# TensorE's order pinned to the written order through the whole retention of a hybrid decoder block

## The chip, the cores and the metric

The kernel runs on one core of one Trainium2 chip. The metric is the device time of one execution in microseconds. Before the change it is 1546.49 us, the median of 3 runs (1546.46 to 1546.75). Everything is float32 data of one sequence of 1024 tokens, model width 1024, one layer.

## What is computed

The layer normalises x, makes one combined projection, runs two branches on it (a retention with 4 heads, and a sliding-window attention), merges them through gates and ends with a SwiGLU feed-forward. The change lies in the retention. There the sequence is cut into 8 chunks of 128 tokens, and a state of 128 x 256 is carried from chunk to chunk:

```python
def step(state, inp):
    qn, kn, vn = inp
    scores = jnp.einsum('bhcd,bhsd->bhcs', qn, kn) * intra_decay
    inner = jnp.einsum('bhcs,bhse->bhce', scores, vn)
    cross = jnp.einsum('bhcd,bhde->bhce', qn, state) * q_decay
    new_state = state * chunk_decay + jnp.einsum('bhsd,bhse->bhde', kn * k_decay, vn)
    return new_state, inner + cross
...
ry = head_group_norm(ry, ret_norm_g[l]).astype(x.dtype)
branch_a = (jax.nn.silu(rg) * ry) @ w_ret_out[l]
...
branch_b = ay.reshape(B, S, ATTN_Q) @ w_attn_out[l]
merged = jax.nn.sigmoid(gate_a) * branch_a + jax.nn.sigmoid(gate_b) * branch_b
```

## The kernel before

Every large product keeps float32 accuracy by splitting each operand into a high part (a cast on ScalarE, `nc.scalar.copy`) and a low part (a subtraction on VectorE), and by three TensorE products (high x high, high x low, low x high) that add up in one PSUM bank. So each value that leaves PSUM and enters a product again passes ScalarE and then VectorE.

The stage around the change is the retention, which follows a stage of weight products (`wproduct`, L1022). That stage ends with results of the gates: `wresult` (L975) adds two parts on VectorE (L1002), takes a tanh on ScalarE (L1009) and stores the result to HBM (L1010, issued from SyncE's queue). Its result tile `r` has two buffers, so the add of one block waits until the store of the block two before has landed. In the same place the second half of the attention result, `ay`, is loaded in two transfers of 2048 KB each (L1048).

Then comes, for head 0, `load_g(0)` and `k_transpose(0)` (L1156): 8 transposes on TensorE into the two banks of PSUM tag `t` (tiles `kTT`), each bank then cast by ScalarE (L1165) and subtracted by VectorE (L1166). Only after both has the bank been read for the last time.

Each head is a generator `core(h)` (L1168 to 1305). Its steps on TensorE are: `scores` (L1194, tile `rs`, a bank of tag `t`), four times `states` (L1185 to 1187 into tile `u`), four times `outputs` (the same lines, into tile `y`), twice `gated` (transposes `yT`, L1258, bank `t`), and `k_transpose` of the next head. `scores` first runs four matmuls into its bank; VectorE multiplies them with the mask (L1197, `sm`), and the halves `smh`, `sml` go into `outputs`. Between the steps the generator yields a number, 3 or 4.

The yields are filled by `Fill` (L208) with the products of `w_attn_out` (`bb_g`, L1141; lines 178 to 180, tile `acc_bb`). A filling step is three matmuls of 128 x 512. There are 8 x 16 = 128 of them, and the yields of the four heads ask for 4 x 32 = 128. They need only `ay` and their own weights `wh_bb`, `wl_bb`, not the retention.

What sets the order: each engine runs its own list of instructions strictly in its order. A scheduler makes that list from the written program, by its own estimate of when operands are ready. Where the code stands within `in_order(engine)` (L117), each instruction of that engine is tied to the one before it as written, and the scheduler can move nothing there. Before, `pinned = in_order(nc.tensor.engine)` opens at L1107 and closes at L1309, just after `k_transpose(0)`. From there on the scheduler chooses TensorE's order. VectorE, ScalarE and SyncE's queue are left to the scheduler in the retention in both kernels.

Of the kernel before, what the change touches and what calls it, by code (L numbers as in the profile page):

```python
# [40 lines left out]
def hybrid_block(ctx: ExitStack, tc: tile.TileContext, x, ln1_g, w_in, b_in, ret_norm_g, w_ret_out,  # L41
# [74 lines left out]
    @contextmanager  # L116
    def in_order(*engines):  # L117

        traced = nc.cur_bb.bb.instructions
        last = traced[-1]  # L120
        yield
        start = next(k for k in reversed(range(len(traced))) if traced[k] is last) + 1
        prev = {}
        for i in traced[start:]:
            if i.engine in engines:
                if i.engine in prev:
                    tc.add_manual_dep(i, prev[i.engine],
                                      mybir.DependencyInfo(mybir.DependencyClass.NoSync, mybir.DependencyReason.DATA),
                                      reason="in_order")
                prev[i.engine] = i.name  # L130
# [53 lines left out]
    def run(gen):  # L184
        for _ in gen:
            pass
# [920 lines left out]
    pinned = in_order(nc.tensor.engine)  # L1107
# [33 lines left out]
    def bb_g(n):  # L1141
        def evac(half, pt):
            c = slice(half * 512, half * 512 + 512)
            t = rt.tile([P, 512], F32, tag="r", bufs=2, name=f"tbr{n}{half}")
            nc.sync.dma_start(t, tb_d[8 + n, :, c])
            m = w2.tile([P, 512], F32, tag="mbw", bufs=1, name=f"mb{n}{half}")
            nc.vector.scalar_tensor_tensor(out=m, in0=t, scalar=1.0, in1=pt, op0=ALU.add, op1=ALU.mult)
            nc.sync.dma_start(mb_d[n, :, c], m)
        return dense_g(w_attn_out, n * P, AY, evac, f"bb{n}")
# [6 lines left out]
    def k_transpose(h):  # L1156
        kt = [w2.tile([P, NB, P], F32R, tag=f"kt{z}", bufs=1, name=f"kt{h}{z}") for z in range(2)]
        kts[h] = kt
        for q in range(2):
            pt = ps("t", 2, f"kTT{h}{q}")  # L1160
            for i in range(4):
                nc.tensor.transpose(pt[:, i * P:(i + 1) * P], kTs[h][:, (q * 4 + i) * P:(q * 4 + i + 1) * P], ident)
            ptv = pt.rearrange("p (c d) -> p c d", c=4)
            hi, lo = (z[:, q * 4:q * 4 + 4, :] for z in kt)
            nc.scalar.copy(hi, ptv)  # L1165
            nc.vector.tensor_tensor(out=lo, in0=ptv, in1=f32(hi), op=ALU.subtract)  # L1166
# [139 lines left out]

    load_g(0)
    k_transpose(0)
    pinned.__exit__(None, None, None)  # L1309
    fl = Fill([bb_g(n) for n in range(8)])  # L1310
    last = None
    for h in range(RH):
# [10 lines left out]
        last = gen  # L1323
    fl.rest()
    run(last)
    w2c.__exit__(None, None, None)
    rtc.__exit__(None, None, None)
    kqc.__exit__(None, None, None)
# [804 lines left out]
```

## Time and profile before

| | before |
|---|---|
| time, median of 3 runs | 1546.49 us |
| the profiled execution, its own time | 1546.24 us |
| its span, first to last instruction | 1544.1 us |
| TensorE (PE) busy | 1532.1 us, 99% |
| VectorE (DVE) busy | 1024.5 us, 66% |
| ScalarE (ACT) busy | 693.5 us, 45% |
| GpSimd (POOL) busy | 386.3 us, 25% |
| mean granted TensorE clock | 0.999 |

The profile is one execution taken by the hardware profiler. Times in its timeline are microseconds from the start of the span. In a row of the timeline stand the start, the duration, the engine, the line of the kernel, the operation, output and inputs, the shape, and in brackets the idle time before it with what ended it. PEld is TensorE's weight load, SPq is SyncE's queue of DMA issues. A matmul is listed with its whole passage, so the spacing of the starts, not the duration, is what it takes from the engine. An `x8` on four float32 matmuls of 128 x 128 means that each is carried out as two.

### The profile page before, as it was taken

The numbers are of one execution on the slowest core, as the hardware profiler recorded it, in microseconds if no ns is written. First come the engines' busy times: TensorE is split into PE (matmuls) and PEld (weight loads), VectorE is DVE, ScalarE is ACT, GpSimd is POOL, SyncE is SP. The second block draws the span as 40 slices with busy tenths as digits, with TensorE's granted clock in tenths as the row PEclk, the third lists the DMA queues.
The fourth block names the chain that finished last, engine by engine and source line by source line (L and its number), as shares of the span: only waits on it lengthen the run. The fifth ranks groups of instructions, "written<-read, shape, count | busy, mean of one in ns | idle before, by whom it ended". The sixth has DMA issues, their size and how long they took to land.

```text
span 1544.1 us, 20386 instructions
## 1 busy us (share of the span) xinstructions
PE 1532.1 (99%) x7299; PEld 1279.8 (83%) x7299; DVE 1024.5 (66%) x1590; ACT 693.5 (45%) x1368; POOL 386.3 (25%) x344
## 2 busy tenths in 40 slices
PE   9999999999999999999999999999999999999998
PEld 8888878888888888888888888888888888888886
DVE  7588897884677764887558688444444444688666
ACT  6366666332344454544223465333333333344445
POOL 2011111002233320000120216555555555100001
PEclk9999999999999999999999999999999999999999
DMA  6656474315766647653657103333333333963332
GB/s 229 187 163 189 144 250 166 103 55 175 207 195 196 213 163 262 206 192 117 204 178 253 68 1 123 109 103 103 102 103 103 103 104 108 318 226 96 92 111 118
DMA packets 158001, 236.85 MB, mean 153 GB/s; under 512 B 10603, under 2 KB 81069, under 8 KB 157645
## 3 DMA queue, kind: packets, MB, share of 16 engines
q1 hardware_dynamic: 155292, 227.04, 45.7%
q0 software_dynamic: 2560, 8.39, 1.5%
q8 instruction: 57, 0.93, 0.3%
q14 instruction: 44, 0.35, 0.1%
q10 hardware_dynamic: 48, 0.13, 0.0%
HBM read 156.62 MB, written 74.19 MB: 149 GB/s over the span
## 4 chain that ended last, share of the span: by engine, by line
PE 94%; DVE 3%; DMA 1%; issue 1%; ACT 1%; SPq 0%; POOL 0%; POOLq 0%; DVEq 0%
PE fA L1757 16%; PE wA L1022 8%; PE fB L1757 8%; PE dA L2059 7%; PE dxP L2059 6%; PE wB L1022 4%; PE fC L1757 4%; PE va L865 3%; PE wo L1591 3%; PE woP L1591 2%; PE wC L1022 2%; PE vP L865 2%; PE aq L178 2%; PE aq L179 2%; PE aq L180 2%; PE acc_ba L180 2%
## 5 line engine op out<-in xcount | busy, mean ns | idle before, releaser
L2059 PE MATMUL dA<-dwP,daP 128*128 128x512 f32 x528 | 120.6, 389 | 0.0
L2059 PEld LDWEIGHTS dA<-dwP,daP 128*128 128x128 f32 x528 | 99.0, 188 | 20.7 <-DVE dwP L154 0.2
L2059 PE MATMUL dxP<-dwP,daP 128*128 128x512 f32 x396 | 90.2, 389 | 0.0
L2059 PEld LDWEIGHTS dxP<-dwP,daP 128*128 128x128 f32 x396 | 74.3, 188 | 15.4
L1832 POOL TENSOR_TENSOR xf<-xf 128x512 f32<-128x512 f32 x40 | 63.9, 1598 | 31.0 <-issue 28.8
L734 POOL TENSOR_TENSOR wr_wp<-wr_wp 128x512 f32<-128x512 f32 x12 | 18.2, 1514 | 193.5 <-DVE w0P L154 92.5
L642 POOL DMA_DIRECT2D xy_d<-xy x32 | 23.1, 723 | 157.2 <-ACT xy L641 98.9
L1763 POOL TENSOR_TENSOR xf<-xf 128x512 f32<-128x512 f32 x33 | 47.3, 1435 | 58.9 <-ACT xf L1765 26.9
L1964 POOL TENSOR_TENSOR rs_f<-tot,mhalf 128x1 f32<-128x1 f32 x8 | 4.9, 607 | 205.4 <-DVE tot L1961 205.4
L154 DVE TENSOR_TENSOR dwP<-wd,dwP 128x512 fp32r<-128x512 f32 x77 | 52.8, 685 | 4.8 <-ACT dwP L151 4.8
L607 ACT ACTIVATE sc<-sc,nm 128x129 f32<-128x129 f32 x128 | 50.1, 402 | 3.6 <-DVE nm L599 3.3
L151 ACT CAST dwP<-wd 128x512 fp32r<-128x512 f32 x77 | 47.4, 616 | 9.1 <-PE dA L2059 6.9
L178 PE MATMUL acc_bb<-ay,wh_bb 128*128 128x512 f32 x128 | 51.0, 400 | 0.0
L151 ACT CAST daP<-daP 128x512 fp32r<-128x512 f32 x42 | 26.0, 621 | 54.8 <-PE dxP L2059 26.7
L180 PE MATMUL acc_bb<-ay,wl_bb 128*128 128x512 f32 x128 | 50.3, 393 | 0.0
L178 PE MATMUL acc_g<-h,wh_g 128*128 128x512 f32 x128 | 50.3, 393 | 0.0
L179 PE MATMUL acc_bb<-ay,wh_bb 128*128 128x512 f32 x128 | 50.2, 392 | 0.0
L178 PE MATMUL aq<-h,wh_aq 128*128 128x512 f32 x128 | 50.2, 392 | 0.0
L179 PE MATMUL aq<-h,wh_aq 128*128 128x512 f32 x128 | 50.0, 391 | 0.0
L179 PE MATMUL acc_g<-h,wh_g 128*128 128x512 f32 x128 | 50.0, 391 | 0.0
L734 POOL TENSOR_TENSOR wr_f<-wr_f 128x512 f32<-128x512 f32 x20 | 30.7, 1533 | 77.2 <-DVE t_6P L154 8.6
L178 PE MATMUL acc_ba<-yg,wh_ba 128*128 128x512 f32 x128 | 49.9, 390 | 0.0
(866 smaller groups left out, 4314.5 us busy)
## 6 DMA issues: line engine op xcount, KB each, us to landing
act_d<-xf SPq DMA_DIRECT2D x77, 256.0 KB, 2.1
daP<-act_d SPq DMA_DIRECT2D x21, 512.0 KB, 3.9
q<-q_d SPq DMA_DIRECT2D x32, 256.0 KB, 4.0
xy_d<-xy POOLq DMA_DIRECT2D x32, 256.0 KB, 3.8
wr_daP<-act_d SPq DMA_DIRECT2D x14, 512.0 KB, 6.7
wr_wp<-in_w_in SPq DMA_DIRECT2D x12, 512.0 KB, 5.4
wp<-in_w_in SPq DMA_DIRECT2D x12, 512.0 KB, 5.2
wd<-in_w_ffn_down SPq DMA_DIRECT2D x6, 1024.0 KB
```

The source lines that it names most:

```text
L151: nc.scalar.copy(hi, raw)
L154: return nc.vector.tensor_tensor(out=lo, in0=raw, in1=f32(hi), op=ALU.subtract)
L178: nc.tensor.matmul(pt, hi[:, k, :], xh, start=(k == 0), stop=False)
L179: nc.tensor.matmul(pt, hi[:, k, :], xl, start=False, stop=False)
L180: nc.tensor.matmul(pt, lo[:, k, :], xh, start=False, stop=(k == 7))
L607: nc.scalar.activation(sc[:, j, 0:P + 1], sc[:, j, 0:P + 1], AF.Exp, scale=-1.0, bias=nm[:, j:j + 1], accum_out=den[:, j:j + 1])
L865: nc.tensor.matmul(vbanks[pr][tt], x_[:, c], w[:, u, :], start=(fresh and k + z == 0), stop=(k == 3 and z == 2), skip_group_check=not fresh)
L1022: nc.tensor.matmul(pt, o[:, w, k, :], v, start=(first and k + z == 0), stop=(k == 3 and z == 2), skip_group_check=not first)
L1591: nc.tensor.matmul(bank, v[:, q + u, k, c], w[y][:, k % 2, :], start=(first and z == 0), stop=(last and z == 2), skip_group_check=not tracked)
L1757: nc.tensor.matmul(pt, o[:, w, k, :], v, start=(first and n == 0), stop=(n == 11), skip_group_check=not first)
L1832: nc.gpsimd.tensor_tensor(out=o, in0=a, in1=b, op=op)
L2059: nc.tensor.matmul(banks[tt], a[:, u, c], w[:, v, :], start=(fresh and f + z == 0), stop=(f == NP - 1 and z == 2), skip_group_check=not fresh)
```

## The change

The line that ends the pinned order moves from ahead of the loop over the heads to behind it:

```diff
     load_g(0)
     k_transpose(0)
-    pinned.__exit__(None, None, None)
     fl = Fill([bb_g(n) for n in range(8)])
...
     fl.rest()
     run(last)
+    pinned.__exit__(None, None, None)
     w2c.__exit__(None, None, None)
```

No instruction is added or taken away. TensorE's list in the retention is now the written one: a step, three or four filling steps, the next step.

The first place is the start of head 0 on TensorE. In this piece of the difference `kTT00` and `kTT01` are the two transposed banks of head 0's k, `rs00` is head 0's first `scores`, and `acc_bb0_0` is the first filling product.

```order
 L1162 MATMUL kTT00_5551<-ident_86,r00_5024 128x128 x4
 L1162 MATMUL kTT01_5558<-ident_86,r00_5024 128x128 x4
+L1194 MATMUL rs00_5566<-r10_5026,r00_5024 128x128 x4
 L178 MATMUL acc_bb0_0_5591<-ay0_4845,wh_bb0_5587 128x512
 L179 MATMUL acc_bb0_0_5591<-ay0_4845,wh_bb0_5587 128x512
```

The first `scores` now stands directly behind the two transposes, ahead of every filling step. In the order before it stood behind 44 filling matmuls; the next piece, also TensorE, is that place, some 45 rows further on, with the names as above, `u00` the first `states` and `rs01` the second `scores`.

```order
-L1194 MATMUL rs00_5566<-r10_5026,r00_5024 128x128 x4
-L1185 MATMUL u00_5601<-vh00_5577,kt00_5549 128x256
-L1194 MATMUL rs01_5748<-r10_5026,r00_5024 128x128
-L1186 MATMUL u00_5601<-vl00_5578,kt00_5549 128x256
-L1187 MATMUL u00_5601<-vh00_5577,kt01_5550 128x256
```

These rows are gone from there; before, the steps of head 0 came late, close together and partly mixed (a matmul of the second `scores` stands inside the first `states`). Similar mixing, of a few matmuls each, is undone in the rest of head 0 and at the start of head 1. From there on TensorE's two lists agree: the scheduler had left the rest of head 1 and heads 2 and 3 as written.

The second place is VectorE at the same point, where the two kernels have the same order through all the rows shown here. They are rows of the changed kernel, with what each waits for; `r1101` is the last gate block of the stage before, `kt01` is the low part of head 0's transposed k.

```order
L1002 TENSOR_TENSOR r1101_5537<-wB11_5453,u211_5447 128x512 [waits DMAHW4_49]
L1166 TENSOR_TENSOR kt01_5550<-kTT00_5551,kt00_5549 128x512 [waits DVE_49,Activation_49]
L1166 TENSOR_TENSOR kt01_5550<-kTT01_5558,kt00_5549 128x512 [waits Activation_49]
L1207 SCALAR_TENSOR_TENSOR vl00_5578<-rv00_5352,rcol_87,vh00_5577 128x512 [waits Activation_49]
L738 TENSOR_TENSOR ql00_5582<-r10_5026,qh00_5581 128x256 [waits Activation_49]
```

Nothing moved in these rows: the subtractions that free the two `t` banks stand behind the add of the last gate block, and that add waits for a DMA. On ScalarE the tanh of that block stands ahead of the casts of `kTT00` and `kTT01` in the same way.

## The prediction

> **What bounds the kernel now.** I read the page first: the engines' busy time and the chain that ended last.
>
> ```profile
> PE 1532.1 (99%) x7299; PEld 1279.8 (83%) x7299; DVE 1024.5 (66%) x1590; ACT 693.5 (45%) x1368; POOL 386.3 (25%) x344
> ...
> PE 94%; DVE 3%; DMA 1%; issue 1%; ACT 1%; SPq 0%; POOL 0%; POOLq 0%; DVEq 0%
> ```
>
> TensorE (PE) is busy for 1532.1 of 1544.1 us, and 94% of the last chain is its work. So two things follow: a stall of TensorE that this kernel doesn't have is added to the end nearly in full, since nothing later stands idle to take it back, and a reordering can gain only what TensorE loses now. How much that is in the retention, the view of the stretches tells: head 0, head 1 and head 2, each from its first `scores` to that of the next head (head 0 from the transposes of its k on). The columns are the stretch, its length, the busy time of PE, PEld, DVE, ACT and POOL, the granted clock, and the DMA engines' share.
>
> ```profile
> 597.72:632.97 35.25, 35.08 (x203) 29.74 (x202) 25.43 (x61) 17.83 (x36) 2.12 (x3) 1.00 0.80 272
> 632.97:667.86 34.89, 34.57 (x204) 30.13 (x203) 29.07 (x73) 17.20 (x34) 3.51 (x5) 1.00 0.55 183
> 667.86:702.44 34.58, 34.55 (x203) 30.28 (x202) 27.41 (x66) 16.66 (x33) 2.78 (x5) 1.00 0.56 185
> ```
>
> TensorE idles 0.17, 0.32 and 0.03 us in them. Head 2, which already runs in the written order, is the template: it shows that the order as such keeps TensorE full while VectorE is busy 27.41 of 34.58 us. What the template doesn't show is how head 0 begins, and there I took the timeline of all engines.
>
> ```profile
> 593.17 0.43 SPq L1048 DMA_DIRECT2D ay<-ay_d  x1
> ...
> 595.69 3.85 SPq L1010 DMA_DIRECT2D tb_d<-r  x2
> ...
> 597.72 1.03 PE L1162 MATMUL kTT<-ident,r 128*128 128x128 f32 x8
> 597.98 1.23 DVE L154 TENSOR_TENSOR wl_bb<-wr_bb,wh_bb 128x1024 fp32r<-128x1024 f32 x1 [3.08 <-PE wB L1022]
> ...
> 598.51 0.48 PE L178 MATMUL acc_bb<-ay,wh_bb 128*128 128x512 f32 x1
> ...
> 599.29 0.39 PE L178 MATMUL acc_bb<-ay,wh_bb 128*128 128x512 f32 x1
> ...
> 599.52 0.39 PE L179 MATMUL acc_bb<-ay,wh_bb 128*128 128x512 f32 x1
> ...
> 599.62 1.51 SPq L167 DMA_DIRECT2D wr_bb<-in_w_attn_out  x2
> ...
> 604.42 0.69 DVE L1002 TENSOR_TENSOR r<-wB,u 128x512 f32<-128x512 f32 x1 [5.22 <-DMA tb_d<-r]
> ...
> 605.20 0.72 ACT L1009 ACTIVATE r<-r,bhalf 128x512 f32<-128x512 f32 x1 [6.01 <-DVE r L1002]
> ...
> 605.83 1.05 ACT L1165 CAST kt<-kTT 128x512 fp32r<-128x512 f32 x2
> ...
> 606.43 1.29 DVE L1166 TENSOR_TENSOR kt<-kTT,kt 128x512 fp32r<-128x512 f32 x2 [1.31 <-ACT kt L1165]
> ...
> 608.59 1.05 PE L1194 MATMUL rs<-r,r 128*128 128x128 f32 x8
> ```
>
> The transposes of k end at about 598.5. Their two banks are emptied only 7 to 9 us later: VectorE waits 5.22 us, up to 604.42, for a store of the gate stage to land (issued at 595.69, behind the `ay` loads), then come the add, the tanh on ScalarE and only then the casts of k at 605.83 and the subtractions at 606.43. Now this costs nothing, because TensorE multiplies filling products from 598.51 to 608.59, one every 0.23 us (599.29 to 599.52). They are the cover that the change takes away.
>
> **The change, part by part.** First, the new wait. `scores` writes a bank of tag `t`, which has two; both hold `kTT`. It takes the bank of the first, whose last reader is the first of the two subtractions. That one starts at 606.43; two take 1.29 us, so one ends at about 607.1, and with the time that a semaphore takes the matmuls of `scores` start at about 607.2. In the old order TensorE would have gone on at 598.5. **Stall: 607.2 - 598.5 = 8.7 us.** Pinned behind `scores` stands everything that TensorE has: all 128 filling steps, which are ready, and all four heads. None of it can pass. Nothing of what ends the wait depends on TensorE's new order: the stores, the `ay` loads and the weight loads up to here are issued by 601.1 and wait for nothing that TensorE does after 598.5, and the rows of VectorE and ScalarE ahead of the subtraction stand as they stood. The filling work isn't saved for later either: 128 steps are asked for by the yields and 128 exist, so what was done under the cover must now be done afterwards, at TensorE's full price.
>
> How the DMA explains the wait is seen in the table of issues for 585 to 612 us:
>
> ```profile
> ay<-ay_d SPq DMA_DIRECT2D x2, 2048.0 KB, 10.5
> ```
>
> The store issued at 595.69 is behind up to 4 MB that take 10.5 us to land; it lands 8.7 us after its issue. That queue is the same in both kernels.
>
> Second, the gain from undoing the mixing. The rows for it are the first `scores` of heads 1, 2 and 3, and in head 2 what its predecessor's last `gated` adds.
>
> ```profile
> 632.97 1.06 PE L1194 MATMUL rs<-r,r 128*128 128x128 f32 x8
> ...
> 667.86 1.05 PE L1194 MATMUL rs<-r,r 128*128 128x128 f32 x8
> ...
> 670.81 1.04 PE L1258 MATMUL yT<-ident,yn 128*128 128x128 f32 x8
> 671.61 0.36 PE L1185 MATMUL u<-vh,kt 128*128 128x256 f32 x1
> ...
> 674.47 0.28 PE L1185 MATMUL y<-vh,smh 128*128 128x256 f32 x1
> ...
> 702.44 1.05 PE L1194 MATMUL rs<-r,r 128*128 128x128 f32 x8
> ```
>
> Head 2 takes 702.44 - 667.86 = 34.58 us. Head 0 has no predecessor's `gated`, which takes 671.61 - 670.81 = 0.80 and some 0.08 for the change of shape; in the written order it needs 33.7 us. Now its work takes 632.97 - 598.51 = 34.46, so 0.76 is gained. Head 1 takes 34.89 and becomes 34.58: 0.31. **Gain: 1.1 us**, the idle times of 0.17 and 0.32 included. More can't come out of the heads' order.
>
> Does head 0 run without new waits after its late start? VectorE still has its second subtraction and `vl`, `ql`, `vl` of head 0 to do, some 2.2 us up to about 609.3; `sm`, the cast `smh` and `sml` follow one another.
>
> ```profile
> 607.63 0.75 DVE L1207 SCALAR_TENSOR_TENSOR vl<-rv,rcol,vh 128x512 fp32r<-128x512 f32 x1
> 608.29 0.42 DVE L738 TENSOR_TENSOR ql<-r,qh 128x256 fp32r<-128x256 f32 x1
> ...
> 609.68 0.69 DVE L1197 TENSOR_TENSOR sm<-rs,rmask 128x512 f32<-128x512 f32 x1 [0.96 <-PE rs L1194]
> ...
> 610.40 0.62 ACT L737 CAST smh<-sm 128x512 fp32r<-128x512 f32 x1 [1.69 <-DVE sm L1197]
> ```
>
> With some 0.6 each, `sml` is there at about 611.2. `outputs` asks for it at 607.2 + (674.47 - 667.86 - 0.88) = 612.9. That is 1.7 us of spare, so I cost it at nothing. The loads that move on SyncE's queue are those of head 1's k and q, its mask, the gate tiles `tbr` and v. In head 1 the same loads stand in the written order:
>
> ```profile
> 649.29 0.32 SPq L1105 DMA_DIRECT2D r<-rk_d  x1
> ...
> 660.06 1.03 PE L1162 MATMUL kTT<-ident,r 128*128 128x128 f32 x8
> ```
>
> Issued 10.8 us ahead of the transposes, k comes without a wait there, so nothing is added; without that cover it would be the landing time past 10.8 us.
>
> Third, TensorE after a pause. No row shows TensorE idle for 8 us within the work, but the start of the kernel shows it after a rest: the warming matmuls of 128 columns, then two products of 512 (four entries), then warming ones again. The columns are the shortest, median and longest duration in ns, and the first and last start.
>
> ```profile
> L290 PE MATMUL warm<-wk x36: 286/311/311, 1.0 to 4.7; 128*128 128x128 bf16 x36
> ...
> L289 PE MATMUL g<-wk x4: 592/592/713, 5.0 to 6.4; 128*128 128x512 f32 x4
> ...
> L290 PE MATMUL warm<-wk x8: 219/219/219, 6.8 to 7.2; 128*128 128x128 bf16 x8
> ```
>
> A row of the view of stretches has the granted clock there, the figure ahead of 0.93:
>
> ```profile
> 3.00:4.00 1.00, 1.00 (x13) 1.00 (x11) 0.75 (x2) 0.00 (x0) 0.00 (x0) 1.00 0.93 328
> ```
>
> The first 36 follow one another every 3.7/35 = 0.106 us, the last 8 every 0.4/7 = 0.057: half the rate up to 6.4 to 6.8 us, then the full one, although the granted clock reads 1.00. So the slow stretch lasted 5.4 to 5.8 us, and half of it, 2.7 to 2.9, was lost. After the stall the loss lies between 0 (no drop) and 2.9. I take **2.4 us**, near the only row, a little below it because TensorE resumes with dense 512-column products.
>
> The Trainium skill, "TensorE: Matmul & The Clock Gate", section "What's actually happening", says that half rate is TensorE's default and that sustained activity releases it, so that an idle engine falls back. By that rule this term is there; without it the sum would end at 1553.8 us. The start of this trace agrees in its spacings (0.106 against 0.057), not in its clock column; no row shows a fall in mid-kernel.
>
> **Sum.** 8.7 + 2.4 - 1.1 = +10.0 us on the profiled execution's 1546.24 (span 1544.1 and 2.1 around it): **1556.2 us**. The median of the runs is 0.25 us above that execution, less than I can resolve.
>
> **Rivals.** *The rate doesn't fall.* Then 8.7 - 1.1 = +7.6: 1553.8 us. For it: the clock column never moves. Against it: the spacings at the start. *A new chain of waits in head 0.* If VectorE's list (25.43 us busy in that stretch) comes late beyond the 1.7 us of spare, TensorE pauses again; an idle of 1.5 us more gives 1557.7. Against it: head 2 with 27.41 us idles 0.03. *The other side, not slower: the store lands early.* If it had landed when VectorE became free at 599.2, add, tanh, cast and subtraction (0.7 + 0.7 + 0.6 + 0.7) would free the bank at about 602; the stall is 3.5, the rate may hold, and 1546.24 + 3.5 - 1.1 = 1548.6, which is within 0.2% (3.1 us). It decides at a stall of 4.1 us, that is with a landing at 599.8 instead of 604.4. Against it: the loads ahead of it are issued before TensorE's order differs. *The change doesn't hold the order*, or `scores` gets its bank without the wait: 1545.2 to 1546.2. The order of the changed program speaks against it.
>
> **How the numbers follow.** Forecast with the stall and the lost rate 0.69; no fall of the rate 0.13; a further wait 0.10; early store 0.05; no stall 0.02; 0.01 is left for what none of these covers. The forecast's own range is 8.7 within half a microsecond and 1.4 to 2.9 for the rate: 1554.7 to 1557.2. The range reaches to the first two rivals: 1553.4 to 1557.8. A measurement of this kernel tells about 0.2% from no change. Slower by more than that: 0.69 + 0.13 + 0.10 = 0.92. Within: 0.05 + 0.02 = 0.07. Faster: the 0.01 left, since only 1.1 us is to be had in the heads.
>
> **What would show it.** The timeline of the changed kernel should have TensorE idle from 598.5 to about 607.2 ahead of `rs`, ended by VectorE's `kt`; filling matmuls behind it twice as far apart as 0.23 us for some 3 to 6 us, then at 0.23; the first `scores` of heads 1 and 2 34.6 us apart; no idle above 0.1 us in head 0 otherwise. I am wrong if `rs` starts before 603, if the stall comes back later (the distance from the last `scores` to the end of the span would shrink), or if `outputs` of head 0 waits for `sml` or `stl`.

## The result, and the profile after

The changed kernel takes 1557.44 us, the median of 6 runs (1556.72 to 1560.67); the kernel before took 1546.64 us beside it (6 runs, 1546.46 to 1546.75). The ratio is 1.0073, with a 95% interval of 1.0062 to 1.0084. So it is slower, by some 11 us: the predicted 1556.2 us is 1.2 us too low. The result lies 0.24 us above the forecast's own range of 1554.7 to 1557.2, and inside the wider range of 1553.4 to 1557.8 that the two priced rivals had drawn. The profiled execution of the changed kernel took 1556.72 us, with a span of 1554.6.

First the page of the changed kernel: busy times, then the chain that ended last.

```profile
PE 1533.2 (99%) x7299; PEld 1282.1 (82%) x7299; DVE 1031.8 (66%) x1590; ACT 693.0 (45%) x1368; POOL 383.6 (25%) x344
...
PE 92%; DVE 3%; DMA 2%; ACT 1%; issue 1%; SPq 0%; POOL 0%; POOLq 0%; DVEq 0%; ACTq 0%
```

The same instructions as before, and nearly the same busy time of TensorE (1533.2 against 1532.1 us), in a span that is 10.5 us longer. So the time is almost all idle time of TensorE. Where it lies, the view of the stretches tells: heads 0, 1 and 2, cut as in the prediction (head 0 from its transposes of k, the others from their first `scores`), with the same columns.

```profile
598.54:643.85 45.31, 36.30 (x203) 31.82 (x202) 28.50 (x67) 17.95 (x36) 2.77 (x4) 0.89 0.63 213
643.85:678.33 34.48, 34.48 (x204) 30.29 (x203) 27.47 (x66) 16.66 (x33) 2.70 (x5) 1.00 0.56 185
678.33:712.92 34.59, 34.57 (x204) 30.27 (x202) 27.40 (x66) 16.66 (x33) 2.77 (x5) 1.00 0.56 185
```

Head 0 takes 45.31 us instead of 35.25 and TensorE idles 9.01 us in it; the mean granted clock there is 0.89. Heads 1 and 2 run full, at 34.48 and 34.59 us. What happens in head 0 shows in the timeline of all engines.

```profile
596.50 4.14 SPq L1010 DMA_DIRECT2D tb_d<-r  x2
...
598.54 1.04 PE L1162 MATMUL kTT<-ident,r 128*128 128x128 f32 x8
...
605.84 0.69 DVE L1002 TENSOR_TENSOR r<-wB,u 128x512 f32<-128x512 f32 x1 [5.82 <-DMA tb_d<-r]
...
606.61 0.72 ACT L1009 ACTIVATE r<-r,bhalf 128x512 f32<-128x512 f32 x1 [6.32 <-DVE r L1002]
...
607.24 1.05 ACT L1165 CAST kt<-kTT 128x512 fp32r<-128x512 f32 x2
...
607.84 1.29 DVE L1166 TENSOR_TENSOR kt<-kTT,kt 128x512 fp32r<-128x512 f32 x2 [1.31 <-ACT kt L1165]
...
608.59 2.08 PE L1194 MATMUL rs<-r,r 128*128 128x128 f32 x8 [9.01 <-DVE kt L1166]
...
610.31 0.78 PE L178 MATMUL acc_bb<-ay,wh_bb 128*128 128x512 f32 x1
610.89 0.63 PE L179 MATMUL acc_bb<-ay,wh_bb 128*128 128x512 f32 x1
611.31 0.63 PE L180 MATMUL acc_bb<-ay,wl_bb 128*128 128x512 f32 x1
611.74 0.63 PE L178 MATMUL acc_bb<-ay,wh_bb 128*128 128x512 f32 x1
612.17 0.46 PE L179 MATMUL acc_bb<-ay,wh_bb 128*128 128x512 f32 x1
612.46 0.39 PE L180 MATMUL acc_bb<-ay,wl_bb 128*128 128x512 f32 x1
612.69 0.39 PE L178 MATMUL acc_bb<-ay,wh_bb 128*128 128x512 f32 x1
```

This is the chain of the prediction, link by link: store, add, tanh, cast, subtraction, `scores`. The brackets read backwards from `rs` lead to the DMA. Behind the wait the filling products start 0.43 us apart (611.31 to 611.74), and from 612.46 on 0.23. The stretches of 4 us around it have the reason: the figure behind POOL's is the granted clock.

```profile
598.00:602.00 4.00, 1.58 (x12) 1.16 (x10) 1.23 (x1) 0.69 (x1) 0.00 (x0) 1.00 1.11 458
602.00:606.00 4.00, 0.00 (x0) 0.00 (x0) 0.16 (x1) 0.00 (x0) 0.00 (x0) 0.51 0.94 313
606.00:610.00 4.00, 1.42 (x6) 1.42 (x7) 2.69 (x5) 3.39 (x7) 0.00 (x0) 0.50 1.02 321
610.00:614.00 4.00, 4.00 (x19) 3.40 (x18) 2.42 (x5) 0.74 (x2) 0.00 (x0) 0.71 0.98 330
```

TensorE worked at 1.00 (2.4 GHz) up to the wait; while it stood idle the grant fell to 0.50 (1.2 GHz), and it is back where the slow rows end, after 612.17.

The 10.48 us between the two profiled executions add up so, with the prediction's size beside each term:

| term | from the rows | measured | predicted |
|---|---|---|---|
| wait | `rs` at 608.59; the transposes are through 0.79 after 598.54, that is at 599.33 | +9.26 | +8.7 |
| lost rate | `rs` to the seventh filling product: 612.69 - 608.59 = 4.10; at full rate 0.90 + 6 x 0.23 = 2.28 (in `warm` the same steps take 616.87 - 614.59 = 2.28) | +1.82 | +2.4 |
| head 0 unmixed | 643.85 - 608.59 - 1.82 = 33.44 against 34.46 | -1.02 | -0.76 |
| head 1 unmixed | 34.48 against 34.89 | -0.41 | -0.31 |
| ahead of the retention | transposes at 598.54 against 597.72 | +0.82 | 0 |
| sum | | +10.47 | +10.0 |

The wait is taken by spacing, from 599.33; the bracket's 9.01 counts from 599.58, the end of the transposes as the row lists it. Nothing is given back behind these heads, and nothing more is lost there: from head 2's first `scores` to the end of the span it is 1544.1 - 667.86 = 876.2 us before and 1554.6 - 678.33 = 876.3 after.

### The profile page after: what moved, and what is told of

It reads as the page before. It is cut to its first block, busy times and chain, and to the rows that moved or that the text cites. A ratio compares the mean times of both kernels' runs of the same rounds, so it can differ in the third digit from the quotient of the medians.

```text
span 1554.6 us, 20382 instructions
## 1 busy us (share of the span) xinstructions
PE 1533.2 (99%) x7299; PEld 1282.1 (82%) x7299; DVE 1031.8 (66%) x1590; ACT 693.0 (45%) x1368; POOL 383.6 (25%) x344
## 4 chain that ended last, share of the span: by engine, by line
PE 92%; DVE 3%; DMA 2%; ACT 1%; issue 1%; SPq 0%; POOL 0%; POOLq 0%; DVEq 0%; ACTq 0%
PE fA L1757 15%; PE wA L1022 8%; PE fB L1757 8%; PE dA L2059 7%; PE dxP L2059 6%; PE wB L1022 4%; PE fC L1757 4%; PE va L865 3%; PE wo L1591 3%; PE wC L1022 2%; PE woP L1591 2%; PE vP L865 2%; PE acc_ba L179 2%; PE acc_ba L178 2%; PE acc_ba L180 2%; PE acc_bb L178 2%
## 5 line engine op out<-in xcount | busy, mean ns | idle before, releaser
L180 PE MATMUL aq<-h,wl_aq 128*128 128x512 f32 x128 | 49.9, 390 | 0.0
```

The source lines that it names most:

```text
L180: nc.tensor.matmul(pt, lo[:, k, :], xh, start=False, stop=(k == 7))
```

## Experiments

Each timed kernel ran beside the kernel before on the same chip. In the first group (`again` to `warm`) that took 1546.49 us (15 runs), in the second (`warm9` to `fill14`) 1547.00 (14 runs), in the third (`control` to `best`) 1546.64 (27 runs). My theory: what costs is TensorE's uncovered wait for the bank, made long by the landing of the store, with the fall of the clock on top. Rivals: the written order itself costs something in the heads; the bank alone makes the wait; the store waits for its queue only; the slow products behind the wait have another cause.

**again**: the changed kernel as it is.

> The changed kernel once more, to see how its time spreads. Main theory: TensorE now waits for a store of the gate stage to land (it ended the wait at 605.84 us in the profiled execution), and the landing differs from execution to execution, so the times spread over 1 us and more, with a median of 1557 to 1558 and the first scores at about 608 to 612 us; before the change the same wait lay under filling products and the times stayed within 0.3 us. Rival: the spread of the first six runs (1556.7 to 1560.7) comes from elsewhere; then the first scores start at 608.6 within 0.2 in this profile too while the time is another one.

Measured: 1556.47 us (1555.84 to 1557.10, 5 runs), ratio 1.0065 (1.0053 to 1.0078). The median lies under the expected 1557 to 1558, and the five runs spread over 1.3 us. In its profile the add comes at 605.58, and the loss of rate, reckoned as in the table, is 1.5 us.

```profile
598.01 1.04 PE L1162 MATMUL kTT<-ident,r 128*128 128x128 f32 x8
608.33 2.08 PE L1194 MATMUL rs<-r,r 128*128 128x128 f32 x8 [9.28 <-DVE kt L1166]
...
643.32 1.05 PE L1194 MATMUL rs<-r,r 128*128 128x128 f32 x8
```

The picture is that of the first profile. Head 0 takes 643.32 - 598.01 = 45.31 us, as long as there: the wait is longer and the loss of rate smaller by about as much. The 0.54 us between the two profiled executions (1556.72 and 1556.18) lie ahead of the retention, where the transposes start 0.53 us earlier. So this pair doesn't show that the landing of the store makes the times spread, as I had expected.

**fill16**: the order stays written, but sixteen filling steps stand ahead of it; for them four yields of each head, those behind `states(2)`, behind `outputs(2)` and `scores(1)`, behind `outputs(4)` and behind `states(6)`, are smaller by one.

```diff
     fl = Fill([bb_g(n) for n in range(8)])
+    fl.step(16)
...
         prep(4)
-        yield 4
+        yield 3
```

> 16 filling steps (48 matmuls, about 10.9 us) stand ahead of the first scores, 4 fewer in each head, all of it pinned. Main theory (the cost is the uncovered wait for the t bank, and the lower rate after it): both go away, 1545.0 to 1546.7 us, spread as small as before the change (about 0.3 us), no idle above 0.3 us ahead of the first scores. Rival (the written order itself costs TensorE something in the heads): still 1550 or more.

Measured: 1548.72 us (1547.28 to 1551.01, 11 runs), ratio 1.0015 (1.0006 to 1.0024). Of the 10 us 8 are gone, and with them the fall of the clock (1.00 throughout 598 to 618 us): the wait needs cover, the written order as such doesn't cost 10 us. But the hoped 1545.0 to 1546.7 was missed, and so was the hoped small spread: the runs lie 3.7 us apart. The timeline of TensorE has two waits of over 1 us that the kernel before doesn't have:

```profile
604.36 0.50 PE L178 MATMUL acc_bb<-ay,wh_bb 128*128 128x512 f32 x1 [1.11 <-DMA ay<-ay_d]
...
658.05 0.39 PE L1186 MATMUL y<-stl,qh 128*128 128x256 f32 x1 [1.36 <-DVE stl L738]
```

The first is the seventh filling step, the first one that needs the later of the two `ay` transfers. The scheduler's list had that step later: six steps of the first half, four of the second, then the last two of the first. The second is `outputs(2)` of head 1. I read it so that the three filling steps behind `states(2)` don't cover VectorE's chain there; `best`, below, speaks against that as the only cause.

**rbuf**: the last gate column's results get other buffers, so that the add doesn't wait for the store of two blocks before.

```diff
-        r = (wtile("rr", 3, f"r{j}{half}{y}") if turned
+        r = (wtile("rr", 3, f"r{j}{half}{y}") if turned or j == NW - 1
```

> The gate stage's last four result tiles get three buffers of their own, so the last add need not wait for a store. Main theory: VectorE adds at about 600 us instead of 605.8, the casts and subtractions of k follow, the first scores start at about 602.8: a wait of about 3.5 us instead of 9.3, and the rate falls less or not at all; 1548.8 to 1550.6 us, with a spread below 0.5 us. Rival (the bank is freed late for another reason than the store): 1556 or more.

Measured: 1555.96 us (1555.28 to 1558.09, 4 runs), ratio 1.0064 (1.0050 to 1.0078): a miss. The timeline tells why.

```profile
599.60 0.68 DVE L1002 TENSOR_TENSOR r<-wB,u 128x512 f32<-128x512 f32 x1
...
607.83 1.07 ACT L1165 CAST kt<-kTT 128x512 fp32r<-128x512 f32 x2 [6.74 <-DMA tb_d<-r]
...
609.20 2.07 PE L1194 MATMUL rs<-r,r 128*128 128x128 f32 x8 [9.96 <-DVE kt L1166]
```

The add ran at 599.60 as planned. But by the program `kt` takes over memory of the stage before, and that memory now held the result that was being stored. So the cast waited for the same kind of landing, at another link. The run shows that removing one wait for a store isn't enough here; it doesn't price the wait at L1002 by itself. The lost rate is larger here: the filling products go on 0.43 us apart up to the ninth, at 614.48, which makes 614.48 - 609.20 - 0.90 - 8 x 0.23 = 2.5 us.

**warm**: eighteen float32 products of 512 columns, unused, keep TensorE at work in its wait.

```diff
+    hot = acc("hot")
+    for n in range(HOT):
+        nc.tensor.matmul(hot, ident, kTs[0][:, 0:512], start=True, stop=True)
     fl = Fill([bb_g(n) for n in range(8)])
```

> 18 products whose result nobody reads (512 columns, float32, about 0.46 us each, 8.3 us together) stand between the transposes of k and the first scores; the wait stays, but TensorE works through most of it. Main theory: the filling products behind the scores follow every 0.23 us at once, and the time falls by the 1.8 us that the lower rate cost: 1555 to 1556 us against 1557.4. Rival (the slow stretch is not due to the pause): 1557 to 1558, with spacings of 0.43 us again.

Measured: 1560.95 us (1560.66 to 1562.17, 4 runs), ratio 1.0096 (1.0082 to 1.0109), against an expected 1555 to 1556: a miss. The group of the added products (columns: shortest, median, longest duration in ns, first and last start), one stretch and the rows behind (lines of this kernel are one higher):

```profile
L1312 PE MATMUL hot<-r,ident x36: 592/592/595, 599.1 to 614.2; 128*128 128x512 f32 x36
...
602.00:606.00 4.00, 4.00 (x10) 1.71 (x9) 0.69 (x1) 0.10 (x1) 0.00 (x0) 1.00 0.99 325
...
615.71 0.40 PE L180 MATMUL acc_bb<-ay,wh_bb 128*128 128x512 f32 x1
615.95 0.40 PE L181 MATMUL acc_bb<-ay,wl_bb 128*128 128x512 f32 x1
```

Each product is two entries of 0.43 us, at a granted clock of 1.00: 15.6 us in all, more than the wait they were to fill, so this kernel waits for its own dummy work. Its use lies in the last rows: behind them the filling products follow 0.24 us apart at once. `rs` starts 15.45 us after the first of the products; with the 1.4 us of the table gained by unmixing, 1546.5 + 15.45 - 1.4 = 1560.5 comes within 0.4 us of the measured time without a loss of rate.

**warm9**: nine such products, so that they end ahead of the bank.

> Nine float32 products of 512 columns (18 entries, about 7.8 us by the 0.43 us that such an entry took before) stand between the transposes of k and the first scores, so TensorE works through most of its wait and should be through at about 607.2, one or two microseconds before the bank is free. The products' results are not used. If the loss of rate after the wait comes from the pause, and TensorE's own wait is otherwise unchanged, the granted clock stays at 1.00 in 598 to 614 us, the filling products follow at 0.23 us from the first on, and the kernel takes 1.5 to 2 us less than the changed kernel: 1554.5 to 1555.2 against 1556.5. If the slow products are a consequence of something else (operands, DMA traffic), they stay slow for 3 us and the time stays at 1556.0 to 1557.0.

Measured: 1555.38 us (1553.65 to 1556.07, 5 runs), ratio 1.0052 (1.0040 to 1.0065). The stretches and the end of the wait:

```profile
606.00:610.00 4.00, 2.80 (x14) 1.65 (x14) 2.69 (x5) 3.50 (x7) 0.00 (x0) 1.00 0.97 303
...
608.47 1.16 PE L1195 MATMUL rs<-r,r 128*128 128x128 f32 x8 [1.20 <-DVE kt L1167]
```

`rs` starts at 608.47, as late as in the changed kernel, but TensorE stood only 1.20 us and the clock stays at 1.00. Against the kernel before the cost falls from 10.0 us (`again`) to 8.4. The time is 0.2 us above the expected 1554.5 to 1555.2, beside a kernel before that is 0.5 us slower than in the first group. The intervals of the two ratios overlap, so the 1.6 us are indicated and not settled by the times. The clock is settled: in the views of 4 us it fell to 0.50 in the five profiles in which TensorE stood for 7.57 to 9.96 us (the changed kernel's two, rbuf, storeq and bank), and it stayed at 1.00 in warm, warm9, fill14, fill16, swap and best.

**storeq**: the last gate column's stores go out from GpSimd's queue.

```diff
-            nc.sync.dma_start(tb_d[n, :, c], r)
+            (nc.gpsimd if j == NW - 1 else nc.sync).dma_start(tb_d[n, :, c], r)
```

> The last gate column's four result stores are issued from GpSimd's queue instead of SyncE's, where they stand behind the two 2048 KB loads of ay. Theory A, the store waits for the loads because it is in their queue: it lands 2 to 4 us after its issue, the add at L1002 runs at about 599 to 600, the bank is free at 602 to 603, TensorE stands for 3 to 4 us instead of 9.3, and the time is 1548.5 to 1550.5. Theory B, what the store lacks is bandwidth (the DMA engines are busy with the loads, whatever the queue): it lands as late as before, the wait at L1002 stays at 5 to 6 us, and the time is 1555.5 to 1557.0.

Measured: 1555.73 us (1555.12 to 1556.01, 5 runs), ratio 1.0055 (1.0041 to 1.0068), in the range of theory B. The timeline:

```profile
590.38 0.80 SPq L1048 DMA_DIRECT2D ay<-ay_d  x2
...
593.72 0.59 POOL L1010 DMA_DIRECT2D tb_d<-r  x1 [5.51 <-ACT r L1009]
...
602.07 0.69 ACT L1009 ACTIVATE r<-wA,bhalf 128x512 f32<-128x512 f32 x1 [5.78 <-DMA tb_d<-r]
...
607.61 2.08 PE L1194 MATMUL rs<-r,r 128*128 128x128 f32 x8 [8.23 <-DVE kt L1166]
```

On a queue of its own the store still lands 8.35 us after its issue (593.72 to 602.07), and the wait has moved from VectorE's add to the tanh of the block before. The DMA engines' share is 1.00 in 598 to 602 us. So a store lands late without standing behind the loads in SyncE's queue; that the engines are full with the 4 MB of loads fits. But the edit changes more than the queue. Both `ay` loads now go out at 590.38, ahead of this store, while in the changed kernel the second of them is issued behind it (593.98 behind 593.61), and there the same store lands within 6.00 us, at 599.61. And GpSimd's queue, which the profile lists as another kind (software_dynamic, SyncE's as hardware_dynamic), wasn't priced without the loads. Which of these makes the store late here isn't separated.

**bank**: head 0's first `scores` takes a bank of tag `s`.

```diff
-            pt = ps("t", 2, f"rs{h}{hf}")
+            pt = ps("s" if h + hf == 0 else "t", 2, f"rs{h}{hf}")
```

> Head 0's first scores takes a bank of PSUM tag s instead of one of tag t, so the two banks that still hold the transposed k no longer stop it. If the bank is the only thing that TensorE waits for, the scores and the nine filling products behind them run at once, and the wait is gone: about 1547 us. If the wait is the same chain (store, add, tanh, cast, subtraction) met once more by the next step, then TensorE runs for 3 to 4 us, up to about 602, and stops at the first states (u), whose operands kt and vl come out of the same rows of ScalarE and VectorE at about 608 to 610: idle time of 6 to 8 us ahead of u instead of 9.3 ahead of rs, a low granted clock behind it, and 1554.5 to 1556.2 us.

Measured: 1557.03 us (1555.72 to 1558.11, 5 runs), ratio 1.0063 (1.0051 to 1.0076).

```profile
599.75 1.06 PE L1194 MATMUL rs<-r,r 128*128 128x128 f32 x8
...
610.46 0.55 PE L1185 MATMUL u<-vh,kt 128*128 128x256 f32 x1 [7.57 <-ACT vh L1206]
611.38 0.58 PE L1186 MATMUL u<-vl,kt 128*128 128x256 f32 x1 [0.36 <-DVE vl L1207]
```

The bank is free and `scores` runs at 599.75, yet the kernel gains nothing: three filling steps later TensorE stands 7.57 us ahead of the first `states`, whose operands come out of the same rows of ScalarE and VectorE. The bank is only the first door; the chain behind the store is the wait. The time was missed by about 1 us: the operands came at 610.46, after the forecast 608 to 610, and then the rate stayed low for long; the nine filling products behind `states` are all 0.43 us apart, up to 616.03. From the first `states` to the fifth product of `outputs` it is 617.28 - 610.46 = 6.82 us, of which 0.36 is a wait; the same steps take 620.81 - 617.57 = 3.24 in warm. So 3.2 us of rate are lost here.

**fill14**: fourteen steps ahead, all taken from head 0, as the scheduler had done.

```diff
+    fl.step(14)
...
-            fl.step(n)
+            fl.step(n if h else 2)
```

> Fourteen of the 128 filling steps (42 products, 9.7 us at 0.23 us each) stand ahead of the loop over the heads, and each yield of head 0 asks for two instead of three or four, so that the sum stays 128; heads 1 to 3 are as in the changed kernel. It is near what the scheduler chose before. If the cost of the change is the uncovered wait and nothing else, it is gone: TensorE idles under 0.5 us from 598 to 640 us unless head 0 with fewer filling steps waits for VectorE or ScalarE, and the time is 1545.2 to 1546.5 us, at or a little below the kernel before. If spreading is what head 0 needs (two filling steps don't cover its chains of states and outputs), waits of 1 us or more for stl or sml stand in head 0 and the time is 1547 to 1549 us.

Measured: 1551.20 us (1549.53 to 1553.22, 10 runs), ratio 1.0028 (1.0019 to 1.0037): a miss beyond both ends. The view of TensorE's waits from 596 to 750 us (total, times, longest):

```profile
PE acc_bb L178 <- DMA ay<-ay_d: 1.5, 1, 1.5
PE y L1186 <- DVE stl L738: 1.2, 3, 0.4
PE yT L1258 <- ACT yn L1251: 0.6, 2, 0.4
```

The same early demand for `ay`, and many short waits for VectorE and ScalarE in head 0, whose chains two filling steps don't cover. The kernel before has 0.7 us of waits in the retention in one profile (control2, below) and 0.5 in the other, though its head 0 has about as few filling steps. That the scheduler places single products between the steps, what I had called mixing, may be why; no run separates it.

**swap**: fill16 with the sixteen steps in the scheduler's order, six, four, two, four.

```diff
+        for half, n, last_part in ((0, 6, False), (1, 4, False), (0, 2, True), (1, 4, True)):
+            for _ in range(n):
+                next(gens[half], None)
+            if last_part:
+                evac(half, pts[half])
...
+    bb_g(0, late_g)
-    fl = Fill([bb_g(n) for n in range(8)])
+    fl = Fill([bb_g(n) for n in range(1, 8)])
```

> As fill16 (sixteen filling steps ahead of the loop over the heads, four yields of each head smaller by one), but the sixteen stand in the order that the scheduler had found before: six steps of the first half, four of the second, then the two of the first half that need the later of the two ay transfers, then the rest. If fill16's wait of 1.1 us at 604 us came from asking for that transfer too early, it is gone, the wait of 1.4 us for stl in head 1 stays, and the time is 0.8 to 1.3 us under fill16's in proportion to the kernel before: 1546.9 to 1548.2 for 1546.5 before. If the load only shifts the wait, the time stays within 0.4 us of fill16's.

Measured: 1547.24 us (1546.35 to 1549.87, 11 runs), ratio 1.0007 (0.9998 to 1.0015). The wait for `ay` is gone, which the trace settles. That for `stl` is 0.84 us instead of the expected 1.4. The ratio is 0.0008 (1.2 us) under that of fill16, as expected, but the two intervals overlap.

**best**: as swap, but the yield behind `states(2)` keeps its four steps and the one behind `outputs(6)` gives up one instead.

> As swap, but the yield between states(2) and outputs(2) keeps its four steps in every head, and the one behind outputs(6) gives one instead. If fill16's other wait (1.4 us for stl in head 1) comes from that yield, it goes too, and TensorE idles under 0.5 us from 598 to 737 us: 1545.3 to 1546.7 us for 1546.5 before, that is the written order without its price, level with or just under the kernel before. If VectorE has to be late somewhere (its work is the same), the wait shows at another step, and the time stays at 1547 to 1548.5.

Measured: 1546.37 us (1545.39 to 1548.78, 11 runs), ratio 0.9999 (0.9990 to 1.0008): level with the kernel before. TensorE's waits that are left in the retention:

```profile
655.07 0.39 PE L1196 MATMUL y<-stl,qh 128*128 128x256 f32 x1 [0.70 <-DVE stl L738]
...
736.12 0.33 PE L1268 MATMUL yT<-ident,yn 128*128 128x128 f32 x1 [0.70 <-ACT yn L1261]
```

Line numbers are ten higher here. The time is as expected, the waits aren't: 1.4 us of them instead of under 0.5, as much as in swap (0.8 and 0.6). So the yield behind `states(2)` wasn't their cause, or not alone, and what sets best under swap isn't shown: its intervals overlap with swap's, and this execution reached the transposes 1.04 us earlier than swap's (597.34 against 598.38). best is the written order without its price; it beats the kernel before by nothing that can be told.

**control** and **control2**: the kernel before, for the 0.82 us ahead of the retention.

> The kernel before, unchanged, profiled once more. Every profile of a kernel with the pinned retention shows a wait of 0.5 to 1.1 us of TensorE at 88 to 89 us (s at L584 for VectorE's sc, L594), and reaches the transposes of k at 598.0 to 598.9; the one profile of the kernel before shows no such wait and 597.72. The lists of all engines up to there are the same. If this differs from execution to execution, this profile shows the wait too, or the transposes start between 597.7 and 598.9 without a reason in the order; if it is something that the change does, this profile again shows no wait and 597.6 to 597.8. In both cases the add at L1002 comes 6 to 8 us after the transposes' start and TensorE doesn't wait for it.

> The kernel before once more, for one profile, since the execution profiled as control ran at half the clock nearly throughout. With best, a kernel with the pinned order has reached the transposes of k at 597.34 without the wait at 89 us, so that wait should come and go from execution to execution: this profile may show it or not, and the transposes start between 597.3 and 598.9. The add at L1002 comes 6.5 to 8 us after them, and TensorE shows no wait in 598 to 640 us; the first scores comes at 608 to 610 and the first scores of head 1 at 632.5 to 634.5.

The times of control are those of the kernel before (median 1546.65 us, ratio 1.0001, 0.9992 to 1.0010), but its profiled execution ran at a mean granted clock of 0.625 and says nothing on the question. control2 took 1546.58 us. The rows are TensorE's wait at 88 us, the transposes and the add:

```profile
88.34 1.22 PE L584 MATMUL s<-kst,q 128*128 128x256 f32 x8 [0.21 <-DVE sc L594]
...
597.80 1.04 PE L1162 MATMUL kTT<-ident,r 128*128 128x128 f32 x8
...
604.92 0.69 DVE L1002 TENSOR_TENSOR r<-wB,u 128x512 f32<-128x512 f32 x1 [5.64 <-DMA tb_d<-r]
```

The changed kernel had 1.04 us at the same place:

```profile
89.09 1.22 PE L584 MATMUL s<-kst,q 128*128 128x256 f32 x8 [1.04 <-DVE sc L594]
```

The wait is there in the kernel before too, shorter, and `best`, with the pinned order, has none and reaches its transposes at 597.34. So neither order always has it. But the other ten profiles with the pinned order all have it, with 0.49 to 1.12 us, and reach the transposes at 598.01 to 598.88, while the two usable ones of the kernel before are at 597.72 and 597.80. That it only comes and goes with the execution is thus not shown; a part of the change in it stays open, though the lists up to there are the same.

The add comes 604.92 - 597.80 = 7.12 us after the transposes; in the first profile of before that was 604.42 - 597.72 = 6.70. The short waits of this execution, between 622 and 639 us, weren't expected.

## Why the prediction came out as it did

**The chain and the wait: right.** TensorE idles from 599.33 to 608.59, ended by VectorE's `kt`. That nothing behind could pass, and that the covered work must be done afterwards, held: the wait is in the total in full. fill16 and swap show it by the cover, bank by the door, rbuf and storeq by the store. **The store as its end: right. Why the store is late: open.** I had named its place behind the loads in the queue. storeq shows a landing as late from another queue, so that place isn't the whole reason, if it is one.

**The size of the wait: 9.26 against 8.7. This is the step that failed**, the term that was mis-sized and the bound set on it. "8.7 within half a microsecond" took one execution's landing as a constant; the two profiles of the changed kernel have 9.26 and, from the transposes' end at 598.80 to `rs` at 608.33, 9.53. The chain behind the add was sized rightly: from the add to `rs` it is 608.59 - 605.84 = 2.75 us, and I had 607.2 - 604.42 = 2.78. What was short is the time from the transposes to the add. I had 6.70 us, the only row there was. All eleven profiles with the stores on SyncE's queue and the two buffers have 6.58 (swap), 6.70 (before), 6.85 (warm), 6.95 (fill16), 7.12 (control2), 7.21 (warm9), 7.30 (after), 7.31 (fill14), 7.53 (best), 7.57 (again) and 7.89 (bank): mine was the second shortest. Where TensorE stood still it was 7.30 to 7.89, where it worked 6.58 to 7.53; with three profiles against eight it isn't shown whether its standing still itself makes the landing later.

Nor is it shown that this spread is what spreads the kernel's times. The changed kernel's six runs lie 3.95 us apart, but those of fill16, swap and best, which have the cover, lie 3.4 to 3.7 us apart too.

**The lost rate: there, 1.82 against 2.4, by a misread row.** That the idle time causes it, warm and warm9 show: with TensorE at work there, the clock stayed at 1.00 and the filling products ran at full rate at once. The rule of the Trainium skill, "TensorE: Matmul & The Clock Gate", section "What's actually happening", by which an idle TensorE falls back to half rate, agrees with this trace: 1.00 ahead of the wait, 0.50 in 606 to 610 us. The price I took from the kernel's slow start, which I counted up to 6.4 to 6.8 us, over the four entries of L289 with 592 ns each. `warm` has entries with the same 592 ns at a clock of 1.00. So all but the first of the four were at the full rate, the slow stretch at the start ended at about 5.0 us, and half of it is about 2.0 us. The loss isn't a constant: 1.5 us in again, 1.8 in after, 2.5 in rbuf and by the same reckoning in storeq, 3.2 in bank. The bounds of 1.4 and 2.9 held both profiles of the changed kernel, not that of bank.

**The gain from unmixing: right** (1.43 against 1.1), and `outputs` of head 0 waits for nothing: the only wait of TensorE that the view of waits lists from 596 to 750 us is that of `rs`. The template of head 2 (34.58) is met by heads 1 and 2 (34.48 and 34.59).

**0.82 us ahead of the retention** was in no term: I had put it at nothing. Whether it belongs to the execution or to the change stays open (control2, above).

So the 1.2 us by which 1557.44 lies above the forecast add up, within rounding, to 0.56 too little for the wait, 0.82 ahead of the retention and 0.72 by which the median of the runs lies above the profiled execution, less 0.58 too much for the rate and 0.36 too little for the gain. Within the retention the forecast was 0.38 us too high for this execution. That its errors cancel so nearly is luck: with 2.0 for the rate, the right reading of my row, the sum would have been 1555.8.

A second set of runs gave 1556.47. The rivals are out: with no fall of the clock 1553.8, with an early store 1548.6, with no stall 1545 to 1546. The further wait, at 1557.7, comes nearest to the measured time but is out by the trace, which has no such wait. The forecast's own range was short above because it gave the wait half a microsecond on the word of one row, and nothing to what lies ahead of the retention and between executions.

## What to carry over

Before an order is pinned, look for what the scheduler had put ahead of a waiting step, and in which order: here it covered a wait of 9 us for a store that no row of TensorE showed, and it also asked for a late load last. Work that fills gaps must be placed by when its own operands land, and by how long the chain behind each step is: the written order came back to the scheduler's time (1546.37 against 1546.64 us) with sixteen steps in front and those on the late load put back among them. And when a cover goes, the whole length of the wait is paid: one trace gives one draw of it (here the way to the add took 6.58 to 7.89 us), so the range needs more.

## What the runs showed of the hardware

- The granted clock fell to 0.50 (1.2 GHz) in a wait of TensorE of 9 us in the middle of the kernel (after), and what that cost behind the wait differs: 1.5 us (again) and 1.8 (after) in two executions of the same kernel, 2.5 (rbuf, storeq) and 3.2 (bank) in others. In warm9, where TensorE worked up to 1.20 us ahead of the same step, it stayed at 1.00.
- A float32 product of 512 columns takes two entries of 0.43 us at a clock of 1.00 (warm), against 0.23 us for a filling product.
- A store of 256 KB that was issued behind two loads of 2048 KB landed 8.7 us after its issue from the same queue (before) and 9.3 us (after, 596.50 to 605.84); one that went out from GpSimd's queue while they were under way took 8.35 us (storeq).
